# A mixture-of-experts product by two levels of Strassen-Winograd: VectorE's order by two clocks, weight sums made early

## The chip, the cores and the metric

The kernel runs on one core of a Trainium2 chip. Its metric is the time of one execution on the device in microseconds (us); less is better.

## The reference

Eight experts, 8192 tokens (16 x 512) of 512 features, 2048 outputs. Every token goes through every expert, and the outputs are added with softmax weights.

```python
probs = softmax(router_logits)                       # (16, 512, 8)
output = np.zeros((16, 512, 2048), np.float32)
for e in range(8):
    output += probs[:, :, e:e+1] * np.matmul(x, expert_weights[e])
```

The kernel reads this as one product: the left matrix has 8192 rows of 8 x 512 = 4096 columns (x times the probability of each expert), the right one stacks the experts, 4096 x 2048.

## The kernel before

**Two levels.** The product is split into halves in all three dimensions and done with seven products in place of eight (Winograd's form). The outer seven, P1 to P7, each have a right operand of 2048 x 1024 made from quarters of the weights: P1 takes the quarter 11, P2 21, P3 22, and P5, P6, P7, P4 take the outer sums t1, t2, t3, t4. The tokens make 16 instances: product(r, q) is outer product r of instance q. It is split again by seven (`STEPS` = 1, 5, 6, 2, 7, 3, 4). One *step* is one inner product: eight matmuls of 128 x 128 by 128 x 512 in f16, accumulated in one PSUM bank. So one outer product of an instance takes 7 steps, and needs seven right tiles of 1 MB in SBUF: three blocks of its operand as they are, and the inner sums 5, 6, 7 and 4 of its blocks (`inner_sums`, `sums_at`, one VectorE subtraction of 128 x 4096 each).

**Left operands.** VectorE makes each instance's left operands (`Left.make`): x transposed times a broadcast probability, a 128 x 2048 operation (tile `z`), for two halves; P6 subtracts P5's operand, P7 and P3 subtract two such products (`less`). `queue_s2` and `queue_i` add the inner left sums (tiles `d`, `z`).

**Evacuation.** After each step `post` moves a bank out: by ScalarE as a copy, by VectorE as an addition (`post_on_base`, 128 x 512, tile `h`). A base is an earlier partial result, held in `kept`, in the output in DRAM, or in SBUF, fetched by SyncE (`Base.fetch`). Results are stored by GpSimd's DMA queue; P4 and P3 add to the output by DMA.

**Stages.** `add` makes a stage of one or two products. `run` takes the steps of a pair in turn, so a pair has 14 slots and a single 7. Hooks put with `at(stage, slot, ...)` start loads and queue VectorE tasks. Before: three pairs of P1, eight of P2 with P1, four of P2, one of P5, a single P6, fourteen of P6 with P5, a single P6, a pair of P7, a single P4, fourteen of P4 with P7, a single P4, eight pairs of P3. The first two instances of P1 run ahead of the stages as plain products.

**The order.** Every engine runs its instructions in the order in which the Python code emits them. VectorE's tasks wait in `queue`. In each slot `slack` adds `SLOT` (1.73 us) to a credit and emits tasks while the credit is positive; a task's cost and an evacuation's 0.69 are taken off. If a step needs an operand that isn't made, `need` emits the queue up to it at once, and the credit goes below zero:

```python
def slack():
    credit[0] += SLOT
    while queue and credit[0] > 0:
        queue.popleft().run()
    credit[0] = min(credit[0], SLOT)
```

**Weights.** `cast_block` and `cast_w` load f32 weights as f16 on GpSimd's queue. `wedge` makes halves of t3, t1, t2 (and t4 of one block) from quarters 12 and 22 in the stages of P1 and P2 and stores them in DRAM (`kept_w`); their temporaries come from `zpool`. `retire` fetches the operand of P7, and of P3, in the last stages of the product before it and queues the four sums there; P4's sums are queued in P7's pair.

Of the kernel before, what the change touches and what calls it, by code (L numbers as in the profile page):

```python
# [31 lines left out]
def kernel(  # L32
# [8 lines left out]
    P = 128  # L41
# [22 lines left out]
    wpool = ctx.enter_context(tc.tile_pool(name="wpool", bufs=15))  # L64
    zpool = ctx.enter_context(tc.tile_pool(name="zpool", bufs=9))
    spool = ctx.enter_context(tc.tile_pool(name="spool", bufs=3))
# [64 lines left out]
    def new_w():  # L131
        return wpool.tile([P, K8, NB], f16, name="w", tag="w")

    def new_z():
        return zpool.tile([P, K8, HQ], f16, name="z", tag="z")
# [15 lines left out]
    def kept_w(what, kn):  # L151
        if (what, kn) not in stored:
            stored[what, kn] = dram.tile([P, K8, NB], f16, name=f"wd{what}_{kn[0]}{kn[1]}")
        return stored[what, kn]
# [178 lines left out]
    STEPS = (1, 5, 6, 2, 7, 3, 4)  # L333
    HP = HQ // 2
    queue = deque()
    credit = [0.0]

    class Task:
# [5 lines left out]
        def run(self):  # L344
            self.done = True
            credit[0] -= self.cost
            self.make()

    def need(task):
        while task is not None and not task.done:  # L350
            queue.popleft().run()

    def later(cost, make, first=False):
# [4 lines left out]
    def slack():  # L358
        credit[0] += SLOT
        while queue and credit[0] > 0:  # L360
            queue.popleft().run()
        credit[0] = min(credit[0], SLOT)

# [50 lines left out]
    class Left:  # L414
# [18 lines left out]
        def queue_make(self, k):  # L433
            cost = 1.22 + (2.33 if self.less is not None else 0) + (1.11 if self.of is not None else 0)
            self.task[k] = later(cost, lambda: self.make(k))

        def queue_s2(self):
            def make():
                self.s2 = spool.tile([P, K8, HP], f16, name="d", tag="d")
                tt(self.s2, self.t[0][:, :, ds(HP, HP)], self.t[0][:, :, ds(0, HP)], SUB)  # L440
            self.task["s2"] = later(0.58, make)

        def queue_i(self):
            def make():
                self.i = new_z()
                two = "p k (h t) -> p h k t"
                tt(self.i.rearrange(two, h=2), self.t[1].rearrange(two, h=2),
                   self.s2.unsqueeze(1).to_broadcast([P, 2, K8, HP]), SUB)
            self.task["i"] = later(1.15, make)

# [27 lines left out]
    class Product:  # L478
# [23 lines left out]
        def post_alone(self, p, x, q, b):  # L502
            o = self.o
            if p == 1:
                self.banks["b"] = bank()
                act(nc.scalar.copy(self.banks["b"], x))  # L506
            elif p in (5, 6):
                tn = (1, 1) if p == 5 else (0, 1)
                o[tn] = half()
                act(nc.scalar.copy(o[tn], q if p == 5 else x))  # L510
            elif p in (2, 4):
                o[TN[p]] = half()
                act(nc.scalar.copy(o[TN[p]], b if p == 2 else x))  # L513
            else:
                credit[0] -= 0.69
                tt(o[TN[p]], x if p == 7 else q, o[TN[p]], ADD)

        def post_on_base(self, p, x, q, b):
# [4 lines left out]
            if p == 2:  # L523
                act(nc.scalar.copy(o[tn], b))  # L524
                return
            credit[0] -= 0.69
            if p == 1:
# [71 lines left out]
    def product(r, q, **how):  # L599
# [7 lines left out]
        elif r == 2:  # L607
            if q >= 7:
# [86 lines left out]
    forget(*range(0, 14, 2))  # L695
    rest = [15, 0, 1, 2, 3, 4, 5, 6]
    for i in range(0, 8, 2):
        k = add(product(2, rest[i]), product(2, rest[i + 1]))
        for slot, tn in zip((8, 10, 12, 13), INNER):
            for q in rest[i:i + 2]:  # L700
                if q < 7:
                    fetch_at(k if tn == (1, 0) else k - 1, 3 if tn == (1, 0) else slot, bases[2, q], tn)
# [10 lines left out]
    for q in range(16):  # L713
# [7 lines left out]
    xs.clear()  # L721
    k7 = add(product(7, 0), product(7, 1))
    add(product(4, 0))
    for q in range(1, 15):
        add(product(4, q), product(7, q + 1))
    k4 = add(product(4, 15))
    for q in range(16):
        k = k7 if q < 2 else k7 + q
        for slot, tn in zip((7, 9, 11, 13) if len(stages[k - 1]) == 2 else (2, 3, 5, 6), INNER):
            fetch_at(k - 1, slot, bases[7, q], tn)  # L730
    xs.clear()
    for q in range(0, 16, 2):
        k3 = add(product(3, q), product(3, q + 1))


    def wedge(kn, e):
# [8 lines left out]

        def temp():
            return zpool.tile([P, C, NB], f16, name="z", tag="z")
# [13 lines left out]
        def t2():  # L761
            tt(b, b, a, ADD)
            send("t2", b)

        def t4():
            u = temp()
            tt(u, b21[kn][:, rows, :], b, SUB)
            send("t4", u)
        return casts, [t3, t1, t2] + ([t4] if kn == (0, 1) else [])

    def wedge_at(stage, slot, kn, e, then):
# [7 lines left out]
        def go_on():  # L779
            for make in made:  # L780
                later(1.11, make)
        at(stage, slot, begin)
        at(stage + then[0], then[1], go_on)

    b21 = {}
    made2 = {}

    def cast21(kn):
        b21[kn] = cast_block(21, kn)

    at(0, 0, lambda: cast21((0, 1)))
    wedge_at(0, 4, (0, 1), 0, (0, 13))
    at(0, 10, lambda: cast21((0, 0)))
    wedge_at(1, 2, (0, 1), 1, (1, 3))
    at(1, 6, lambda: cast21((1, 1)))
    at(1, 12, lambda: cast21((1, 0)))

    def sums_at(stage, slot, r, of, ps):
# [5 lines left out]
        at(stage, slot, go)  # L804
    sums_at(2, 5, 2, b21, (5, 6))
    sums_at(2, 10, 2, b21, (7, 4))
    for i, (kn, e) in enumerate((kn, e) for kn in ((0, 0), (1, 0), (1, 1)) for e in range(2)):
        wedge_at(3 + i, 2, kn, e, (0, 11))

    t1, t2, t3, t4, b22 = {}, {}, {}, {}, {}  # L810

    def fetch_at_w(stage, slot, of, what, kn):
        at(stage, slot, lambda: of.__setitem__(kn, fetch_w(what, kn)))
    for i, kn in enumerate(((0, 0), (0, 1), (1, 1), (1, 0))):
        fetch_at_w(11, 3 * i, t1, "t1", kn)
        fetch_at_w(12, 3 * i, t2, "t2", kn)
    last2 = k5 - 1
# [5 lines left out]

    def t4_at(stage, kn):
        def begin():
            t4[kn] = cast_block(21, kn)

        def go_on():
            def make():
                t = t4.pop(kn)  # L830
                tt(t, t, t2[kn], SUB)
                pool(kept_w("t4", kn), t)
            later(2.29, make)
        at(stage, 2, begin)
        at(stage + 1, 2, go_on)
    for i, kn in enumerate(((0, 0), (1, 0), (1, 1))):
        t4_at(k5 + 3 + 2 * i, kn)

    def retire(stage, r, of, fetch):

        order = ((0, 0), (0, 1), (1, 1), (1, 0))
        at(stage - 4, 2, lambda: fetch(order[0]))
        for slot, kn in zip((2, 4, 6), order[1:]):
            at(stage, slot, lambda kn=kn: fetch(kn))
        sums_at(stage, 13, r, of, (5, 6))
        sums_at(stage + 1, 2, r, of, (7, 4))
    retire(k7 - 2, 7, t3, lambda kn: t3.__setitem__(kn, fetch_w("t3", kn)))
    for i, kn in enumerate(((0, 0), (0, 1), (1, 1), (1, 0))):
        fetch_at_w(k7, 1 + i, t4, "t4", kn)
    sums_at(k7, 8, 4, t4, (5, 6))  # L850
    sums_at(k7, 11, 4, t4, (7, 4))
    retire(k4 - 1, 3, b22, lambda kn: b22.__setitem__(kn, cast_block(22, kn)))


    finish = products[3, 15]
    for q in (14, 15):
        p = products[3, q]
        p.base = bases[3, q] = Base(lambda tn, q=q: out_rows(q, 0, 1, tn))
        p.sink = lambda tn, o, q=q: sp(out_rows(q, 0, 1, tn), o)
        for slot, tn in zip((8, 10, 12, 13), INNER):  # L860
            fetch_at(k3 - 1, slot, p.base, tn)
    finish.steps = (1, 5, 6, 7, 3, 4, 2)
# [67 lines left out]
```

## Time and profile before

| | us |
|---|---|
| median of 3 runs | 1533.98 (1532.76 to 1534.71) |
| profiled execution | 1532.25 |
| its span, first to last instruction | 1530.4 |
| TensorE busy | 1406.5 (92%), 6390 matmuls |
| VectorE busy | 1109.0 (72%), 1252 instructions |
| ScalarE busy | 181.2 (12%) |
| GpSimd busy | 349.9 (23%) |

The DMA moved 303.91 MB, 199 GB/s on average. Busy times are shares of one execution, and matmuls overlap in the pipeline: their busy time says when TensorE had work, not how fast it went. In the page's slices each digit is a fortieth of the span, 38.3 us. PEclk is the clock that TensorE was granted. In lists of waits the columns are the sum in us, the number of waits and the longest; in a chain, the start, the length and what ran. L107 is the helper of every VectorE operation, L127 that of every matmul, L121 and L118 those of GpSimd's and SyncE's DMAs; so tiles tell more than lines.

### The profile page before, as it was taken

What the parts mean: (1) busy time and instruction counts of PE and PEld (TensorE: products, weight loads), DVE (VectorE), ACT (ScalarE), POOL (GpSimd) and SP (SyncE); (2) the same over time, 40 slices, a digit from 0 to 9 for tenths busy, and PEclk for the clock granted to TensorE, in tenths of its full rate; (3) what the DMA queues carried; (4) which work ended last, traced back from release to release, by engine and by line L of the source; (5) the groups of instructions that cost most, each with busy time, mean ns of one, the idle gap of its engine ahead of it and who ended that gap; (6) DMA issues with size and microseconds to landing.
All of it is one profiled execution on the core that took longest, in us unless ns stands there. A gap on an engine that the chain in (4) does not pass through costs nothing.

```text
span 1530.4 us, 17248 instructions
## 1 busy us (share of the span) xinstructions
PE 1406.5 (92%) x6390; PEld 627.5 (41%) x6390; DVE 1109.0 (72%) x1252; ACT 181.2 (12%) x314; POOL 349.9 (23%) x547
## 2 busy tenths in 40 slices
PE   9997999999999999999996667678999999789999
PEld 4443444444444444444442222223444444334444
DVE  5857776657788878787767454457998886779983
ACT  3211111100011111111110000000000000112220
POOL 3233332211212222212110101111212214122321
PEclk9998999999999999999998789899999999999999
DMA  9999989689668788766673334445878879678985
GB/s 198 226 296 251 244 265 221 207 304 318 218 191 243 226 240 224 245 212 202 204 262 127 135 83 103 117 117 138 204 203 193 219 186 190 130 126 183 200 171 124
DMA packets 180420, 303.91 MB, mean 199 GB/s; under 512 B 51056, under 2 KB 83056, under 8 KB 177904
## 3 DMA queue, kind: packets, MB, share of 16 engines
q0 software_dynamic: 79712, 163.09, 45.2%
q1 hardware_dynamic: 100624, 139.73, 30.4%
q8 instruction: 50, 0.82, 0.2%
q14 instruction: 34, 0.28, 0.1%
HBM read 185.11 MB, written 142.80 MB: 214 GB/s over the span
## 4 chain that ended last, share of the span: by engine, by line
PE 70%; issue 13%; DVE 10%; DMA 4%; POOL 3%; ACT 0%; POOLq 0%; DVEq 0%; ACTq 0%
PE ps L127 70%; DVE z L107 6%; POOL out_dram L121 2%; DMA w<-in_expert_weights_dram 2%; DVE h L107 2%; DVE w L107 1%; DMA kept<-h 1%; DMA wdt<-z 1%; DVE d L107 1%; POOL xs L121 0%; DMA h<-out_dram 0%; DMA out_dram<-h 0%; POOL w L121 0%; DMA h<-kept 0%; DVE ps L107 0%
## 5 line engine op out<-in xcount | busy, mean ns | idle before, releaser
L127 PE MATMUL ps<-w,z 128*128 128x512 f16 x5416 | 1212.5, 385 | 104.4 <-DVE z L107 82.4
L127 PEld LDWEIGHTS <-z 128*128 128x128 f16 x5416 | 534.7, 99 | 771.3 <-DVE z L107 96.5
L107 DVE TENSOR_TENSOR h<-ps,h 128x512 f32<-128x512 f32 x418 | 283.7, 688 | 328.1 <-PE ps L127 318.9
L121 POOL DMA_DIRECT2D out_dram<-h x376 | 243.8, 674 | 975.3 <-ACT h L524 478.3
L107 DVE TENSOR_TENSOR z<-xT,pT 128x2048 f16<-128x2048 f16 x284 | 339.3, 1218 | 10.1 <-DMA wdt<-z 6.2
L127 PE MATMUL ps<-w,d 128*128 128x512 f16 x880 | 201.8, 381 | 13.2 <-DVE d L107 6.9
L127 PEld LDWEIGHTS <-d 128*128 128x128 f16 x880 | 86.1, 98 | 120.1 <-DVE d L107 9.4
L107 DVE TENSOR_TENSOR z<-z,d 128x2048 f16<-128x2048 f16 x110 | 130.2, 1218 | 0.6 <-DMA wdt<-z 0.6
L107 DVE TENSOR_TENSOR z<-z 128x2048 f16<-128x2048 f16 x96 | 117.6, 1225 | 3.3
L524 ACT COPY h<-ps 128x512 f32<-128x512 f32 x65 | 38.1, 586 | 616.5 <-PE ps L127 615.3
L513 ACT COPY h<-ps 128x512 f32<-128x512 f32 x88 | 51.6, 587 | 382.8 <-PE ps L127 352.6
L107 DVE TENSOR_TENSOR w<-w 128x4096 f16<-128x4096 f16 (+1 forms) x47 | 90.0, 1925 | 0.7
L107 DVE TENSOR_TENSOR d<-z 128x1024 f16<-128x1024 f16 x110 | 75.6, 688 | 8.5 <-PE ps L127 6.3
L510 ACT COPY h<-ps 128x512 f32<-128x512 f32 x88 | 51.6, 586 | 175.1 <-PE ps L127 168.3
L107 DVE TENSOR_TENSOR ps<-ps,h 128x512 f32<-128x512 f32 (+1 forms) x67 | 45.8, 687 | 34.7 <-PE ps L127 32.9
L107 DVE TENSOR_TENSOR h<-h 128x512 f32<-128x512 f32 (+2 forms) x69 | 45.1, 675 | 0.1
L121 POOL DMA_DIRECT2D kept<-h x56 | 30.6, 547 | 50.9 <-DVE h L107 23.2
L121 POOL DMA_DIRECT2D w<-in_expert_weights_dram x47 | 35.5, 768 | 26.3 <-DMA w<-in_expert_weights_dram 11.7
L506 ACT COPY ps<-ps 128x512 f32<-128x512 f32 x44 | 25.1, 570 | 131.5 <-PE ps L127 131.1
L121 POOL DMA_DIRECT2D xs<-in_x_dram x30 | 21.5, 715 | 37.4 <-DMA x<-xT 25.6
L107 DVE TENSOR_TENSOR z<-w 128x2048 f16<-128x2048 f16 x10 | 12.2, 1219 | 13.2 <-DMA wdt<-z 10.1
L121 POOL DMA_DIRECT2D wdt<-w x19 | 10.2, 539 | 48.1 <-DVE w L107 48.1
(43 smaller groups left out, 60.9 us busy)
## 6 DMA issues: line engine op xcount, KB each, us to landing
out_dram<-h POOLq DMA_DIRECT2D x376, 256.0 KB, 4.7
pT<-p_dram SPq DMA_DIRECT2D x140, 256.0 KB, 5.2
h<-kept SPq DMA_DIRECT2D x92, 256.0 KB, 4.2
w<-in_expert_weights_dram POOLq DMA_DIRECT2D x45, 512.0 KB, 10.1
xT<-x SPq DMA_DIRECT2D x85, 256.0 KB, 4.9
h<-out_dram SPq DMA_DIRECT2D x72, 256.0 KB, 5.2
w<-wdt SPq DMA_DIRECT2D x16, 1024.0 KB, 10.0
kept<-h POOLq DMA_DIRECT2D x56, 256.0 KB, 4.7
```

The costliest lines, as they stand in the source:

```text
L107: dve(nc.vector.tensor_tensor(out=o, in0=a, in1=b, op=op))
L121: note(nc.gpsimd.dma_start(out=o, in_=i, **how))
L127: note(nc.tensor.matmul(ps, z, w, start=start, stop=stop, skip_group_check=True))
L506: act(nc.scalar.copy(self.banks["b"], x))
L510: act(nc.scalar.copy(o[tn], q if p == 5 else x))
L513: act(nc.scalar.copy(o[TN[p]], b if p == 2 else x))
L524: act(nc.scalar.copy(o[tn], b))
```

## The change

- The credit becomes two clocks, one for TensorE and one for VectorE. A slot moves TensorE's by 1.73; VectorE's tasks are emitted until its clock is within 0.3 (`LAG`) of TensorE's; neither clock falls behind the other's start, and a forced task moves TensorE's clock on.
- The inner sums of P7, P4 and P3 are made early and kept in DRAM: P7's whole (in a stage of P2), P4's and P3's in quarters (in stages of P6 with P5 and of P4 with P7). `turnover` then fetches seven tiles, one per pair of slots, each into the buffer of the product before whose step has just run.
- The stages: four pairs of P1, six of P2 with P1, five of P2, one of P5, a single P6, fourteen of P6 with P5, P6 with P7, fifteen of P4 with P7, P4 with P3, seven of P3, a single P3.
- Temporaries of the weights and of `less` have one buffer `u` of their own, and `zpool` 8 in place of 9. The block (0, 1) of t4 is made whole, from t2 kept in the buffer of quarter 11. The casts of quarter 21 and the wedges move to other slots.

```diff
-    zpool = ctx.enter_context(tc.tile_pool(name="zpool", bufs=9))
+    zpool = ctx.enter_context(tc.tile_pool(name="zpool", bufs=8))
...
+    def new_u():
+        return zpool.tile([P, K8, HQ], f16, name="u", tag="u", bufs=1)
...
+    LAG = 0.3
     queue = deque()
-    credit = [0.0]
+    clock = {"pe": 0.0, "dve": 0.0}
...
         def run(self):
             self.done = True
-            credit[0] -= self.cost
+            clock["dve"] += self.cost
             self.make()
 
     def need(task):
         while task is not None and not task.done:
             queue.popleft().run()
+            clock["pe"] = max(clock["pe"], clock["dve"])
...
     def slack():
-        credit[0] += SLOT
-        while queue and credit[0] > 0:
+        clock["dve"] = max(clock["dve"], clock["pe"])
+        clock["pe"] += SLOT
+        while queue and clock["dve"] < clock["pe"] - LAG:
             queue.popleft().run()
-        credit[0] = min(credit[0], SLOT)
+
+    def evacuated():
+        clock["dve"] = max(clock["dve"], clock["pe"]) + 0.69
...
             if self.less is not None:
-                u = new_z()
+                u = new_u()
...
-    for q in (2, 4, 6):
+    for q in (2, 4, 6, 8):
         add(product(1, q), product(1, q + 1))
-    for q in range(7, 15):
+    for q in range(9, 15):
         add(product(2, q), product(1, q + 1))
...
-    add(product(6, 15))
+    some = product(6, 15)
+    xs.clear()
+    k7 = add(some, product(7, 0))
+    for q in range(15):
+        add(product(4, q), product(7, q + 1))
+    some = product(4, 15)
+    xs.clear()
+    k3 = add(some, product(3, 0))
+    for q in range(1, 15, 2):
+        add(product(3, q), product(3, q + 1))
+    end = add(product(3, 15))
...
+        for slot, tn in zip((7, 9, 11, 17), INNER):
+            fetch_at(k7 + q - 1 + slot // 14, slot % 14, bases[7, q], tn)
...
         def t3():
-            u = temp()
+            u = new_u().rearrange("p (c two) t -> p c (two t)", two=2)
             tt(u, b, a, SUB)
             send("t3", u)
...
-    at(0, 0, lambda: cast21((0, 1)))
     wedge_at(0, 4, (0, 1), 0, (0, 13))
-    at(0, 10, lambda: cast21((0, 0)))
-    wedge_at(1, 2, (0, 1), 1, (1, 3))
-    at(1, 6, lambda: cast21((1, 1)))
-    at(1, 12, lambda: cast21((1, 0)))
+    at(0, 11, lambda: cast21((0, 1)))
+    wedge_at(1, 2, (0, 1), 1, (1, 11))
+    at(1, 8, lambda: cast21((0, 0)))
+    at(2, 2, early_t4)
+    at(2, 3, lambda: cast21((1, 1)))
+    at(2, 10, lambda: cast21((1, 0)))
...
-    sums_at(2, 5, 2, b21, (5, 6))
-    sums_at(2, 10, 2, b21, (7, 4))
+    sums_at(3, 1, 2, b21, (5,))
+    sums_at(3, 4, 2, b21, (6,))
+    sums_at(3, 7, 2, b21, (7,))
+    sums_at(3, 10, 2, b21, (4,))
...
+    def sums_in_place(part, b, r, cost):
+
+        def one(p, o, x, y):
+            def make():
+                tt(o, x, y, SUB)
+                part(p, o)
+            later(cost, make)
+        one(5, b[0, 0], b[0, 1], b[0, 0])
+        one(7, b[0, 1], b[1, 1], b[0, 1])
+        one(6, b[1, 1], b[1, 1], b[0, 0])
+        one(4, b[1, 0], b[1, 0], b[1, 1])
...
+    for i, kn in enumerate(ORDER):
+        fetch_at_w(10, 1 + 3 * i, t3, "t3", kn)
+        fetch_at_w(12, 1 + 3 * i, t1, "t1", kn)
+        fetch_at_w(13, 1 + 3 * i, t2, "t2", kn)
+    at(11, 2, lambda: whole_sums(7, t3))
...
+        t4_at(*slots_after(k5 + 2, 4, 20 * i), kn)
+    sums_by_parts(*slots_after(k5 + 2, 4, 62), 20, 4,
+                  lambda t, kn, j, chunks: sp(t, kept_w("t4", kn)[:, chunks, :]))
+    sums_by_parts(k7 + 4, 4, 36, 3, cast_part)
+
+
+    RAW = {1: (0, 0), 2: (1, 0), 3: (1, 1)}
+
+    def turnover(stage, place, r, raw):
+
+        right[r].w = {}
+
+        def fetch(p):
+            if p in RAW:
+                right[r].w[p] = raw(RAW[p])
+            else:
+                right[r].w[p] = new_w()
+                sp(right[r].w[p], kept_w((r, p), (0, 0)))
+        at(stage - 1, 9, lambda: fetch(1))
+        for i, p in enumerate(STEPS[1:]):
+            at(stage, place + 2 * i + 1, lambda p=p: fetch(p))
+    turnover(k7 - 1, 1, 7, lambda kn: fetch_w("t3", kn))
+    turnover(k7, 0, 4, lambda kn: fetch_w("t4", kn))
+    turnover(k3 - 1, 1, 3, lambda kn: cast_block(22, kn))
```

More of the change, by code (lines that the diff above doesn't have):

```diff
@@ L152, in kept_w @@
         if (what, kn) not in stored:
-            stored[what, kn] = dram.tile([P, K8, NB], f16, name=f"wd{what}_{kn[0]}{kn[1]}")
+            stored[what, kn] = dram.tile([P, K8, NB], f16, name="wd")
         return stored[what, kn]
@@ L433, in queue_make @@
         def queue_make(self, k):
-            cost = 1.22 + (2.33 if self.less is not None else 0) + (1.11 if self.of is not None else 0)
+            cost = 1.22 + (2.45 if self.less is not None else 0) + (1.23 if self.of is not None else 0)
             self.task[k] = later(cost, lambda: self.make(k))
@@ L440, in make @@
                 tt(self.s2, self.t[0][:, :, ds(HP, HP)], self.t[0][:, :, ds(0, HP)], SUB)
-            self.task["s2"] = later(0.58, make)
+            self.task["s2"] = later(0.69, make)
         def queue_i(self):
@@ L448, in make @@
                    self.s2.unsqueeze(1).to_broadcast([P, 2, K8, HP]), SUB)
-            self.task["i"] = later(1.15, make)
+            self.task["i"] = later(1.22, make)
         def op(self, p):
@@ L514, in post_alone @@
             else:
-                credit[0] -= 0.69
+                evacuated()
                 tt(o[TN[p]], x if p == 7 else q, o[TN[p]], ADD)
@@ L525, in post_on_base @@
                 return
-            credit[0] -= 0.69
+            evacuated()
             if p == 1:
@@ L607, in product @@
         elif r == 2:
-            if q >= 7:
+            if q >= 9:
                 base = products[1, q].o.__getitem__
@@ L688, in fetch_at @@
             at(stage, slot, lambda tn=tn: base.fetch(tn))
-    for q in (2, 4, 6):
+    for q in (2, 4, 6, 8):
         add(product(1, q), product(1, q + 1))
-    for q in range(7, 15):
+    for q in range(9, 15):
         add(product(2, q), product(1, q + 1))
-    forget(*range(0, 14, 2))
-    rest = [15, 0, 1, 2, 3, 4, 5, 6]
-    for i in range(0, 8, 2):
+    forget(*range(0, 18, 2))
+    rest = [15] + list(range(9))
+    for i in range(0, 10, 2):
         k = add(product(2, rest[i]), product(2, rest[i + 1]))
@@ L700 @@
             for q in rest[i:i + 2]:
-                if q < 7:
+                if q < 9:
                     fetch_at(k if tn == (1, 0) else k - 1, 3 if tn == (1, 0) else slot, bases[2, q], tn)
@@ L720 @@
             at(*where, lambda q=q, tn=tn: joined(q, tn))
[L721 to L733, printed above, removed]
+        for slot, tn in zip((7, 9, 11, 17), INNER):
+            fetch_at(k7 + q - 1 + slot // 14, slot % 14, bases[7, q], tn)
     def wedge(kn, e):
@@ L744, in casts @@
             cast_w(22, kn, e, b)
-        def temp():
-            return zpool.tile([P, C, NB], f16, name="z", tag="z")
         def send(what, u):
@@ L761, in t2 @@
         def t2():
[L762 to L769, printed above, removed]
+            if kn == (0, 1):
+                tt(b11[kn][:, rows, :], b, a, ADD)
+                send("t2", b11[kn][:, rows, :])
+            else:
+                tt(b, b, a, ADD)
+                send("t2", b)
+        return casts, [t3, t1, t2]
     def wedge_at(stage, slot, kn, e, then):
@@ L780, in go_on, with early_t4 @@
             for make in made:
-                later(1.11, make)
+                later(1.22, make)
         at(stage, slot, begin)
-        at(stage + then[0], then[1], go_on)
-    b21 = {}
-    made2 = {}
+        at(*then, go_on)
+    b21, t1, t2, t3 = {}, {}, {}, {}
     def cast21(kn):
         b21[kn] = cast_block(21, kn)
-    at(0, 0, lambda: cast21((0, 1)))
-    wedge_at(0, 4, (0, 1), 0, (0, 13))
-    at(0, 10, lambda: cast21((0, 0)))
-    wedge_at(1, 2, (0, 1), 1, (1, 3))
-    at(1, 6, lambda: cast21((1, 1)))
-    at(1, 12, lambda: cast21((1, 0)))
+    def early_t4():
+        kn = 0, 1
+        def make():
+            t = new_w()
+            tt(t, b21[kn], b11[kn], SUB)
+            pool(kept_w("t4", kn), t)
+        later(2.29, make)
+    wedge_at(0, 4, (0, 1), 0, (0, 13))
+    at(0, 11, lambda: cast21((0, 1)))
[4 more added lines that the diff above has]
+    at(2, 10, lambda: cast21((1, 0)))
     def sums_at(stage, slot, r, of, ps):
@@ L804, in sums_at, with make, whole_sums @@
         at(stage, slot, go)
-    sums_at(2, 5, 2, b21, (5, 6))
-    sums_at(2, 10, 2, b21, (7, 4))
+    sums_at(3, 1, 2, b21, (5,))
+    sums_at(3, 4, 2, b21, (6,))
+    sums_at(3, 7, 2, b21, (7,))
+    sums_at(3, 10, 2, b21, (4,))
     for i, (kn, e) in enumerate((kn, e) for kn in ((0, 0), (1, 0), (1, 1)) for e in range(2)):
-        wedge_at(3 + i, 2, kn, e, (0, 11))
-    t1, t2, t3, t4, b22 = {}, {}, {}, {}, {}
+        wedge_at(4 + i, 2, kn, e, (4 + i, 11))
     def fetch_at_w(stage, slot, of, what, kn):
         at(stage, slot, lambda: of.__setitem__(kn, fetch_w(what, kn)))
-    for i, kn in enumerate(((0, 0), (0, 1), (1, 1), (1, 0))):
-        fetch_at_w(11, 3 * i, t1, "t1", kn)
-        fetch_at_w(12, 3 * i, t2, "t2", kn)
+    ORDER = ((0, 0), (0, 1), (1, 1), (1, 0))
+    def sums_in_place(part, b, r, cost):
+        def one(p, o, x, y):
+            def make():
+                tt(o, x, y, SUB)
[5 more added lines that the diff above has]
+        one(4, b[1, 0], b[1, 0], b[1, 1])
+    def whole_sums(r, b):
+        sums_in_place(lambda p, o: pool(kept_w((r, p), (0, 0)), o), b, r, 2.29)
+    for i, kn in enumerate(ORDER):
[3 more added lines that the diff above has]
+    at(11, 2, lambda: whole_sums(7, t3))
     last2 = k5 - 1
@@ L822 @@
     sums_at(k5, 8, 6, t2, (7, 4))
[L824 to L835, printed above, removed]
-    for i, kn in enumerate(((0, 0), (1, 0), (1, 1))):
[L837 to L852, printed above, removed]
-    finish = products[3, 15]
[L856 to L861, printed above, removed]
+    def slots_after(stage, slot, n):
+        slot += n
+        while slot >= 7 * len(stages[stage]):
+            slot -= 7 * len(stages[stage])
+            stage += 1
+        return stage, slot
@@ new lines, in t4_at, with make, sums_by_parts, begin @@
+    def t4_at(stage, slot, kn):
+        t = []
+        def make():
+            tt(t[0], t[0], t2[kn], SUB)
+            pool(kept_w("t4", kn), t.pop())
+        at(stage, slot, lambda: t.append(cast_block(21, kn)))
+        at(*slots_after(stage, slot, 11), lambda: later(2.29, make))
+    def sums_by_parts(stage, slot, every, r, load):
+        for j in range(4):
+            b, chunks = {}, ds(2 * j, 2)
+            def begin(b=b, j=j, chunks=chunks):
+                t = new_w()
+                for i, kn in enumerate(ORDER):
+                    b[kn] = t[:, ds(2 * i, 2), :]
+                    load(b[kn], kn, j, chunks)
+            def go_on(b=b, chunks=chunks):
+                sums_in_place(lambda p, o: pool(kept_w((r, p), (0, 0))[:, chunks, :], o), b, r, 0.69)
+            at(*slots_after(stage, slot, j * every), begin)
+            at(*slots_after(stage, slot, j * every + 8), go_on)
@@ new lines, in cast_part @@
+    def cast_part(t, kn, j, chunks):
+        k, n = kn
+        pool(t, expert_weights[HE + 2 * k + j // 2, ds(j % 2 * 2 * P, 2 * P),
+                               ds(NH + n * NB, NB)].rearrange("(c p) n -> p c n", p=P))
+    for i, kn in enumerate(((0, 0), (1, 0), (1, 1))):
+        t4_at(*slots_after(k5 + 2, 4, 20 * i), kn)
+    sums_by_parts(*slots_after(k5 + 2, 4, 62), 20, 4,
+                  lambda t, kn, j, chunks: sp(t, kept_w("t4", kn)[:, chunks, :]))
+    sums_by_parts(k7 + 4, 4, 36, 3, cast_part)
@@ new lines @@
+    RAW = {1: (0, 0), 2: (1, 0), 3: (1, 1)}
[4 more added lines that the diff above has]
+                right[r].w[p] = raw(RAW[p])
+            else:
+                right[r].w[p] = new_w()
[4 more added lines that the diff above has]
+    turnover(k7 - 1, 1, 7, lambda kn: fetch_w("t3", kn))
@@ L862 @@
+    turnover(k7, 0, 4, lambda kn: fetch_w("t4", kn))
+    turnover(k3 - 1, 1, 3, lambda kn: cast_block(22, kn))
+    finish = products[3, 15]
+    finish.base = Base(lambda tn: out_rows(15, 0, 1, tn))
+    finish.sink = lambda tn, o: sp(out_rows(15, 0, 1, tn), o)
+    for slot, tn in zip((6, 8, 10, 12), INNER):
+        fetch_at(end - 1, slot, finish.base, tn)
     finish.steps = (1, 5, 6, 7, 3, 4, 2)
```

## The prediction

> **What bounds the kernel now.** I read the page's slices first: TensorE, VectorE, the granted clock.
>
> ```profile
> PE   9997999999999999999996667678999999789999
> DVE  5857776657788878787767454457998886779983
> PEclk9998999999999999999998789899999999999999
> ```
>
> Both engines sag together in slices 22 to 28, so neither is the bound there. Then the table of busy time by stretch (length; busy time and count of TensorE, its weight loads, VectorE, ScalarE, GpSimd; granted clock; DMA share; GB/s):
>
> ```profile
> 65.80:91.70 25.90, 24.27 (x113) 10.91 (x112) 16.61 (x17) 5.83 (x10) 9.68 (x16) 1.00 1.14 297
> 91.70:128.30 36.60, 25.99 (x114) 11.38 (x113) 22.36 (x19) 5.83 (x10) 9.29 (x17) 0.86 1.09 282
> 128.30:442.50 314.20, 314.20 (x1457) 142.41 (x1456) 222.72 (x251) 38.52 (x66) 84.29 (x147) 1.00 0.86 247
> 783.40:810.20 26.80, 24.53 (x114) 10.98 (x113) 18.67 (x21) 2.35 (x4) 5.95 (x11) 1.00 0.74 259
> 810.20:1069.00 258.80, 176.58 (x674) 69.79 (x673) 141.66 (x154) 6.45 (x11) 31.08 (x45) 0.85 0.43 117
> 1069.00:1286.50 217.50, 217.50 (x1009) 98.60 (x1008) 188.18 (x221) 10.55 (x18) 57.08 (x80) 1.00 0.80 196
> 1286.50:1406.00 119.50, 101.03 (x450) 44.43 (x449) 89.80 (x88) 18.66 (x32) 27.65 (x34) 0.96 0.75 151
> ```
>
> Call eight matmuls of one inner product a step. Thirteen pairs of 14 steps took 314.2 us with TensorE always busy: 24.17 us a pair, 1.726 a step, no loss. All 770 steps are 55 pairs. So each stretch has a loss: 41.6 to 128.3 us holds three pairs, 86.7 - 72.5 = 14.2; 442.5 to 469.2 one, 2.5; 783.4 to 810.2 one, 2.6; 810.2 to 1069 six, 258.8 - 145.0 = 113.8; 1286.5 to 1406 four, 22.8. Together 155.9 of the span's 1530.4; with none, 1374.5. Of the 113.8, idling is 82.2 (258.8 - 176.6); the other 31.6 is matmuls at a low clock (176.6 - 145.0).
>
> Now the waits in 810.2 to 1069, and a piece of the chain there:
>
> ```profile
> DVE h L107 <- PE ps L127: 89.2, 52, 4.3
> PE ps L127 <- DVE z L107: 67.5, 23, 6.7
> ```
>
> ```profile
> 857.07 0.69 DVE h L107
> 857.76 1.14 DVE z L107
> 858.91 0.04 issue
> 858.95 1.92 PE ps L127 x8
> ```
>
> VectorE waits for TensorE to evacuate a bank, makes the next operand only behind that, and TensorE waits for it: two engines in turn. The cause is the order in which the program puts VectorE's instructions. Its credit goes negative when operands are forced, and until it is repaid nothing is made ahead.
>
> **The change, part by part.** *VectorE's order.* I walked the compiled order of both kernels. For each step I took the VectorE instruction that makes its operand or frees its bank, and the evacuations ahead of it. Work from an evacuation to the operand was priced by the trace's spacing when VectorE is not waiting (0.60 us an evacuation or half operand, 1.14 a 2048-wide one, 2.20 a whole weight sum; above, 857.76 to 858.91 is one 1.14) and set against 1.726 us for each step TensorE has in between. Before, 59 steps come out late: 44 in the 810-to-1069 stretch, 9 in 1286-to-1406, 4 at 783-to-810, 2 at 442-to-469, where the waits are; none elsewhere. One late pair there (from 959 us) has seven late steps of 2.4, 1.8, 1.8, 1.8, 5.9, 2.4 and 2.0, 18.1 in all; it took 43.10 against 24.17, 18.9. So the count prices well. In the changed order two steps are late: 1.9 us soon after the single of P6 (3.7 of work against 1.73), and 0.7 in the last product. Of the 141.7 us in those four stretches (2.5 + 2.6 + 113.8 + 22.8), 2.6 stays.
>
> *Weight sums.* Twelve whole sums (12 x 2.20 = 26.4 us) at the turnovers become 4 whole and 32 quarter sums (8.8 + 32 x 0.60 = 28.0) in stages with room. What hides them: a pair of P4 and P7 has 19.9 us of VectorE work by these spacings, 22.3 with four quarter sums; a pair of P2 15.3, 24.1 with P7's four. Both stay under 24.17 (one group of 14 steps reaches 24.4, beside one of 17.7); an excess that lasts would be lost pair by pair. Taken: 0.
>
> *Their DMA.* Each of P7, P4 and P3 gets about 11 MB more (stores, loads of sums, and a second read of sources), 33 on 304. The dense spot is P7's turnover: the stage before its pair with P6 issues 7 loads of 1024 KB, 8 stores, 7 base loads and 6 operand loads of 256 KB, 12.25 MB; the next stage 6 loads and 18 transfers, 10.5. That is 23.9 million bytes in 48.3 us. Two stretches show what the DMA can carry, and the page the latencies:
>
> ```profile
> 345.80:370.00 24.20, 24.20 (x114) 10.95 (x113) 15.84 (x20) 1.17 (x2) 4.40 (x9) 1.00 0.99 370
> 325.00:330.00 5.00, 5.00 (x25) 2.25 (x23) 4.62 (x6) 0.00 (x0) 0.00 (x0) 1.00 1.03 419
> ```
>
> ```profile
> h<-out_dram SPq DMA_DIRECT2D x72, 256.0 KB, 5.2
> w<-wdt SPq DMA_DIRECT2D x16, 1024.0 KB, 10.0
> ```
>
> At 419 GB/s the two stages take 57.0 us, 8.7 too long; at 370, 64.6 and 16.3. A weight is fetched 15 steps (25.9 us) ahead and lands in 10.0 or so: 15.9 to spare, enough. The base loads of P7 stand in the same SyncE queue only 8 steps (13.8 us) ahead: 8.6 to spare, so at 370 GB/s they come up to 7.7 late. VectorE's evacuation, and every operand behind it in its order, would wait; TensorE feels it after about three steps (5.2 us). Ends: 0 (8.7 just fits) and 16.3 (the whole backlog); I take 4, nearer to the row of 419, since the fetches are large.
>
> Here a rule speaks against the change. The Trainium skill, "DMA: Bandwidth & Descriptors", Specifications, gives some 358 GB/s as the HBM limit of a core; by it the two stages would take 66.8 us and the estimate for this term would be 18.5. The stretch of 345.8 to 370 ran at 370 without any loss, and 419 was seen, so the trace speaks for less.
>
> Four stages of P2 now carry 9.0 to 9.5 MB each (P7's sums, then t1 and t2): 38.3 million bytes in 96.7 us, 396 GB/s. At 419 nothing is lost, at 370 6.8; I take 1.5, as a light stage (3.5 MB) follows. P3's turnover: as many bytes as before (8.75 MB against 7.75 a stage), where the walk explains all the loss; 1, ends 0 and 5.
>
> *The start.* Waits in 91.7 to 128.3:
>
> ```profile
> DVE z L107 <- DMA wdt<-z: 10.8, 2, 10.1
> PE ps L127 <- DVE h L107: 10.6, 1, 10.6
> ```
>
> An operand's buffer was still being stored as a weight temporary, VectorE stood 10.1 us, and TensorE 10.6 behind it. The change gives the temporary a buffer of its own, so this wait goes. It also spreads the casts (four per stage, not six in one) and starts P2 a stage later. What is late next: the DMA stays full (share 1.14 and 1.09), and the second wedge's casts have 9 steps, 15.5 us, to land, against a median of 13.0 between 40 and 135 us in this trace. If they are late, VectorE stands at t3 with evacuations behind it. Ends: 0 and 14.2 (as before); I take 3. Two casts leave the prologue; TensorE was busy 38.7 of its 41.6 us, so at most 1 us is gained: 0 taken, 1 kept for the low end. The pool of operands shrinks from 9 to 8, but the temporaries that shared it left: 0.
>
> *Clock.* The slow stretch ran at 0.85 with idle gaps up to 6.7 us; at 448 us a gap of 2.3 left it at 1.00 (442.5 to 469.2 lost no more than that). Single gaps of 1.9 and 0.7 therefore cost only themselves. The skill's "TensorE: Matmul & The Clock Gate", Part 1, has half rate after an idle window of about 3.4 us; by it too these two would cost nothing more, while a DMA wait of 5 us would bring, as an estimate, 1.7 us on top.
>
> **Sum.** 1374.5 + 2.6 + 4 + 1.5 + 1 + 3 = 1386.6 us of span. The profiled execution took 1532.25 for a span of 1530.4, 1.85 around it; the median, 1533.98, is 1.73 above it. So 1386.6 + 3.6 = 1390.2.
>
> **Rivals.** *DMA pays it back at P7's turnover:* base loads late by the whole 16.3 instead of 4: 1402. For it: 12.25 MB in one stage was never tried. Against: 419 GB/s. *The start stays as it was* (14.2 in place of 3): 1401. For it: share 1.14 there. Against: the wait named is on a buffer that goes. *The order does not hold:* the clocks count no DMA wait, so one late load sets VectorE behind its evacuations again; six pairs at 18.1 are 109 more: 1499. Against: the new clocks forgive debt, so the next pair starts even. *Slower than before:* the same alternation, but lasting in the 29 pairs of P4, P7 and P3, where VectorE is fullest (19.6 to 24.4 of 24.17) and has least room to catch up; 18.1 a pair, so from nine pairs on the gain is gone; at twelve, 1390 + 217 = 1607. Against: 1069 to 1286, with the same 20 us of work a pair, lost nothing once it was even.
>
> **Chances.** Forecast 0.63 (1379 to 1396), turnover 0.15, start 0.12, order not held 0.07, slower 0.03. The range: low, all DMA terms at 0 and 1 gained at the prologue, 1374.5 + 2.6 - 1 + 3.6 = 1379.7; high, all at their upper ends, 1374.5 + 2.6 + 16.3 + 6.8 + 5 + 14.2 + 3.6 = 1423. That leaves out 0.10. A difference under 0.2%, 3 us, can't be told from none: faster 0.96, same 0.01, slower 0.03.
>
> **What would show it.** Right: the stretch from 800 us on at 24.17 a pair, clock 1.00, and hardly any wait of TensorE for z. Wrong: waits for z in P4 and P7 pairs (order), waits of VectorE for h from out_dram at P7's turnover (DMA), or of TensorE before 130 us (start). A time over 1425 would mean that the walk missed a wait.

## The result, and the profile after

The changed kernel took 1418.01 us (median of four runs, 1416.24 to 1419.3) against 1533.74: a ratio of 0.9245, interval 0.9229 to 0.9261. The forecast was 1390, range 1379 to 1423. The profiled execution took 1416.24 for a span of 1414.4.

The slices of TensorE, VectorE and the granted clock no longer sag in the middle:

```profile
PE   8998999999989999999999899999999999899998
DVE  4956767669679888887877688888888986798882
PEclk9999999999999999999999999999999999999999
```

The table by stretch, cut where steps were lost (columns as before):

```profile
91.20:123.60 32.40, 26.09 (x114) 11.36 (x113) 20.24 (x20) 5.84 (x10) 10.24 (x17) 0.95 1.16 279
389.50:419.90 30.40, 26.03 (x113) 11.39 (x112) 21.49 (x23) 1.17 (x2) 3.30 (x7) 0.94 0.89 301
444.00:470.70 26.70, 24.51 (x114) 10.84 (x112) 25.32 (x31) 2.92 (x5) 5.74 (x10) 1.00 1.01 239
784.90:817.30 32.40, 26.69 (x114) 11.48 (x112) 20.94 (x27) 1.76 (x3) 4.34 (x8) 0.89 0.98 380
817.30:1180.70 363.40, 362.77 (x1682) 164.35 (x1680) 316.07 (x377) 17.62 (x30) 107.66 (x156) 1.00 0.86 228
1180.70:1240.60 59.90, 51.31 (x226) 22.47 (x224) 44.47 (x48) 8.17 (x14) 14.67 (x19) 0.94 1.00 249
1240.60:1409.90 169.30, 168.52 (x786) 76.63 (x784) 129.45 (x132) 37.40 (x64) 48.26 (x56) 1.00 0.79 159
```

The fifth row is what the change did: fifteen pairs of P6, P4 and P7 in 363.40 us, 24.23 a pair, where six took 258.8 before. The other rows are what stayed. The first four hold one pair of 24.17 each and the sixth two, so they lost 8.2, 6.2, 2.5, 8.2 and 11.6 us. With 0.8 each at 66 to 91 and 841 to 866, and 0.9 in the last product (in the last row, where TensorE idles for 0.8), that is 39.2 of the span, against 155.9 before.

VectorE's waits for a DMA tell what most of them are (sum in us, number, longest):

```profile
DVE h L107 <- DMA out_dram<-h: 15.8, 7, 7.6
DVE z L107 <- DMA xT<-xs: 14.8, 3, 6.3
DVE h L107 <- DMA h<-kept: 9.9, 1, 9.9
DVE ps L107 <- DMA h<-kept: 9.9, 2, 8.7
DVE h L107 <- DMA h<-out_dram: 8.9, 2, 6.9
```

Beside these it waits 217 times for a bank from TensorE (199.7 us, which cost nothing while TensorE is busy), 10.9 us for ScalarE before the stages begin, and twice near 100 us, which the profile puts down to issue (7.6) and to TensorE (6.6); both are taken up below, under the start. TensorE's wait for z, 67.5 us before in the slow stretch alone, is down to one of 2.2, at P6's single.

### The profile page after: what moved, and what is told of

Same layout as the page of the kernel before. It is cut to its first block, busy times and chain, and to the rows that moved or that the text cites. A ratio compares the mean times of both kernels' runs of the same rounds, so it can differ in the third digit from the quotient of the medians.

```text
span 1414.4 us, 17403 instructions
## 1 busy us (share of the span) xinstructions
PE 1377.9 (97%) x6390; PEld 624.0 (44%) x6390; DVE 1105.4 (78%) x1271; ACT 183.8 (13%) x318; POOL 383.8 (27%) x600
## 4 chain that ended last, share of the span: by engine, by line
PE 81%; DMA 11%; DVE 3%; issue 2%; SPq 1%; POOL 1%; ACT 0%; DVEq 0%; POOLq 0%; ACTq 0%
PE ps L127 81%; DMA h<-kept 3%; DMA w<-in_expert_weights_dram 2%; DMA xT<-xs 2%; DMA out_dram<-h 2%; DMA h<-out_dram 1%; SPq L393 1%; DVE h L107 1%; DVE z L107 1%; DMA xs<-in_x_dram 1%; DMA xT<-x 1%; DMA w<-wd 1%; POOL w L121 0%; DVE w L107 0%; POOL out_dram L121 0%
## 5 line engine op out<-in xcount | busy, mean ns | idle before, releaser
L127 PE MATMUL ps<-w,z 128*128 128x512 f16 x5416 | 1182.6, 380 | 17.8 <-DVE h L107 15.4
L121 POOL DMA_DIRECT2D out_dram<-h x380 | 248.6, 679 | 838.0 <-ACT h L532 433.6
L107 DVE TENSOR_TENSOR z<-xT,pT 128x2048 f16<-128x2048 f16 x220 | 267.1, 1218 | 21.3 <-DMA xT<-xs 14.8
L127 PE MATMUL ps<-w,d 128*128 128x512 f16 x880 | 203.1, 384 | 11.6 <-DVE ps L107 11.6
L107 DVE TENSOR_TENSOR w<-w 128x1024 f16<-128x1024 f16 (+2 forms) x72 | 96.0, 1336 | 0.5
L107 DVE TENSOR_TENSOR z<-z,u 128x2048 f16<-128x2048 f16 x64 | 78.4, 1225 | 2.2
L107 DVE TENSOR_TENSOR u<-xT,pT 128x2048 f16<-128x2048 f16 x64 | 78.0, 1219 | 0.0
L121 POOL DMA_DIRECT2D w<-in_expert_weights_dram x61 | 46.1, 775 | 31.3 <-PE ps L127 11.6
L107 DVE TENSOR_TENSOR h<-h 128x512 f32<-128x512 f32 (+2 forms) x69 | 45.0, 675 | 11.7 <-DMA h<-kept 9.9
L121 POOL DMA_DIRECT2D wd<-w x56 | 31.3, 559 | 39.3 <-DVE w L107 32.2
L107 DVE TENSOR_TENSOR z<-z 128x2048 f16<-128x2048 f16 x32 | 39.2, 1225 | 1.1
```

The lines of the kernel that those rows point to most:

```text
L107: dve(nc.vector.tensor_tensor(out=o, in0=a, in1=b, op=op))
L121: note(nc.gpsimd.dma_start(out=o, in_=i, **how))
L127: note(nc.tensor.matmul(ps, z, w, start=start, stop=stop, skip_group_check=True))
```

## The experiments

In the table, the us lost to the 24.17 cadence at each place, from each kernel's one profiled execution, and the median of its runs. The column of P2 counts all from 300 to 420 us; the 0.9 of the last product is left out.

| kernel | start | P2, 300-420 | P6 single | to P7 and P4 | to P3 | median |
|---|---|---|---|---|---|---|
| before | 14.1 | 0 | 2.5 | 116.4 | 22.7 | 1533.7 |
| changed | 9.0 | 6.2 | 2.5 | 9.0 | 11.6 | 1418.0 |
| clocks only | 11.7 | 0 | 2.5 | 17.4 | 12.2 | 1421.9 |
| old credit | 9.8 | 7.4 | 2.5 | 8.7 | 12.8 | 1420.6 |
| singles | 7.9 | 6.9 | 2.5 | 9.0 | 15.6 | 1421.6 |
| singles, old credit | 9.4 | 8.0 | 2.5 | 9.5 | 11.7 | 1419.7 |
| bases first | 8.6 | 1.5 | 5.0 | 8.8 | 12.3 | 1414.4 |
| raw f16 | 7.4 | 6.6 | 2.5 | 9.1 | 0 | 1403.9 |
| ScalarE's queue | 8.9 | 6.7 | 2.5 | 5.1 | 8.8 | 1407.5 |
| start | 11.6 | 6.9 | 2.5 | 9.0 | 11.8 | 1418.7 |
| three together | 6.5 | 7.6 | 2.5 | 5.4 | 5.6 | 1405.4 |
| three and start | 12.8 | 4.2 | 2.5 | 4.8 | 5.2 | 1409.5 |
| three and P7's bases | 7.4 | 5.5 | 4.1 | 8.1 | 5.6 | 1408.2 |
| bases first, raw f16 | 8.6 | 2.1 | 3.3 | 8.8 | 0 | 1401.0 |

**Which part brought it.** Four kernels undo or do single parts. The clocks, with the task costs of after (0.07 to 0.12 us higher each), in the kernel before; from the edit:

```diff
...
     def slack():
-        credit[0] += SLOT
-        while queue and credit[0] > 0:
+        clock["dve"] = max(clock["dve"], clock["pe"])
+        clock["pe"] += SLOT
+        while queue and clock["dve"] < clock["pe"] - LAG:
             queue.popleft().run()
-        credit[0] = min(credit[0], SLOT)
...
```

> The kernel before with the two clocks (and the changed task costs) alone; singles, late weight sums and the start stay as they were. Theory A, the one on record: the credit's debt is the cause, so the two clocks bring most of the gain. The walk over this kernel's order still leaves 25 late steps with 47.9 us, at the turnovers to P7 and P4 (17.3 and 12.6) and to P3 (11.6), where 171 us were late before. So 1534 - 141.7 + 48 = 1440 us, somewhat more where gaps over 3 us bring the half clock, say 1440 to 1460. Theory B, the sums at the turnovers are the cause whatever the order: little gained, over 1490.

Measured 1421.91, ratio to before 0.9272 (0.9253 to 0.9291). The clocks bring nearly all of the gain, more than theory A's 1440 to 1460 gave them. The stretch in which before lost 116 us, and TensorE's wait for z from 800 to 1250 us:

```profile
808.80:871.80 63.00, 50.85 (x226) 21.94 (x224) 57.68 (x59) 1.76 (x3) 8.34 (x13) 0.95 0.62 198
871.80:1186.10 314.30, 314.30 (x1458) 142.47 (x1456) 270.37 (x318) 15.25 (x26) 79.86 (x112) 1.00 0.76 192
```

```profile
PE ps L127 <- DVE z L107: 23.1, 8, 7.3
```

At the turnover VectorE is busy 57.7 of 63.0 us: the sums fill it, TensorE waits for z, and then it is over. Before, the alternation went on for four more pairs. The Python code of before gives the course of its credit: it falls to -12.5 us, stays below zero from P6's last single to the sixth pair of P4 with P7, and tasks are forced in each stage from P7's pair to the fourth of these pairs. With the higher task costs and the old credit it would fall to -13.8 and stay below zero for longer, so the costs aren't what helped.

The reverse, the changed kernel with the old credit (the same edit turned around, with the task costs of before):

> The changed kernel with the credit and the task costs of before in place of the two clocks; early sums, pairs and the start as changed. Theory A (the credit's debt is the cause): the alternation comes back, 1480 us or more. Theory B (the sums at the turnovers are what makes the debt, and without them either order does): the walk finds 3 late steps with 3.4 us against 2 with 2.6, so within 5 us of 1418.

Measured 1420.61, ratio to before 0.9264 (0.9245 to 0.9284). Theory A falls in the form that went on record: with the sums out of the turnovers the credit, by the code, never falls below -3.4 us, is back at its upper bound of 1.73 within every pair from P6 with P7 on, and forces no task there. TensorE waits for VectorE nowhere between 820 and 1182 us:

```profile
819.70:1182.60 362.90, 362.79 (x1682) 164.37 (x1680) 316.29 (x379) 17.58 (x30) 107.73 (x156) 1.00 0.88 228
```

Then the pairs. The stages of before from P6 on, first with the clocks, then with the credit too:

```diff
-    some = product(6, 15)
+    add(product(6, 15))
     xs.clear()
-    k7 = add(some, product(7, 0))
-    for q in range(15):
+    k7 = add(product(7, 0), product(7, 1))
+    add(product(4, 0))
+    for q in range(1, 15):
         add(product(4, q), product(7, q + 1))
...
```

> The changed kernel with the stages of before from P6 on (single P6, a pair of P7, single P4 at both ends, eight pairs of P3); clocks, early sums and the start as changed. If the pairs in the middle matter by VectorE's order: the walk finds 9 late steps with 13.5 us against 2.6, so 1418 + 11 = 1429. If what matters there is the DMA at the turnovers, it goes the other way: with a whole stage more between fetch and use the stalls of 8 us at P7's and 11 us at P3's turnover shrink, and the sum stays near 1418 or falls below.

> The singles of before and the credit of before, with the early weight sums (and the start) of the change: what the early sums do without the other two. Walk: 10 late steps with 12.2 us. Theory B (early sums alone are the gain): 1418 to 1432. Theory A: 1480 us or more.

Measured 1421.61 and 1419.70 (ratios 0.9265 and 0.9254, intervals 0.9248 to 0.9283 and 0.9233 to 0.9275). So the singles cost nothing that can be told; the stalls at the turnovers didn't shrink either (9.0 and 15.6 us, for 9.0 and 11.6 in the changed kernel). And the early sums (with the changed start), with credit and singles, bring the gain as well. Clocks and early sums are two remedies for one loss: either takes the alternation away, and the second finds little left. In exchange, the early sums bring DMA: the clocks-only kernel loses nothing at 390 to 420 us.

**What the changed kernel still loses.** Four kernels change one thing each. Base loads of one stage ahead of the transposes:

```diff
-        for slot, tn in zip((8, 10, 12, 13), INNER):
+        for slot, tn in zip((2, 4, 5, 6) if i == 8 else (8, 10, 12, 13), INNER):
```

> The changed kernel; in the last stage but one before P5's pair (the stage of P2's instances 5 and 6) the eight base loads are put at slots 2, 4, 5, 6 in place of 8, 10, 12, 13, ahead of the transposes of P5's x in SyncE's queue. Theory: the 6.2 us lost at 390 to 420 us come from base loads that stood behind transposes, which stood 20.4 us for x to land. Then that loss goes, and 1418 becomes 1412. Rival: the DMA engines are full there (9 to 9.5 MB a stage) and any order in the queue loses the same: 1418, the loss at another step.

Measured 1414.35, and 1.5 us lost there in place of 6.2: the order in SyncE's queue was the cause. The seven kernels of the table with the early sums and without this edit lost 6.2 to 8.0 there; of the whole times the intervals just overlap (0.9203 to 0.923, and 0.9229 to 0.9261). Some of it came back at P6's single (5.0 for 2.5). The reason named was not quite right. SyncE's issues in the changed kernel, and VectorE's wait there:

```profile
376.70 12.27 SPq L393 DMA_TRANSPOSE xT<-xs  x4
...
389.72 2.25 SPq L118 DMA_DIRECT2D h<-kept  x4
```

```profile
DVE ps L107 <- DMA h<-kept: 8.7, 1, 8.7
```

SyncE was busy for 12.3 us with issuing four transposes whose x had landed, and the base loads behind them came late, 10.4 us after issue. The wait of 20.4 us for x is another: it began at 407.8 us, when the loss was over.

P3's raw blocks as f16 from DRAM:

```diff
+    def copy_raw(stage, kn, e):
+        at(stage, 8, lambda: cast_w(22, kn, e, kept_w("raw", kn)[:, ds(e * C, C), :]))
+    for stage, (kn, e) in zip((1, 2, 3, 5, 8, 10), ((kn, e) for kn in RAW.values() for e in range(2))):
+        copy_raw(k7 + stage, kn, e)
...
-    turnover(k3 - 1, 1, 3, lambda kn: cast_block(22, kn))
+    turnover(k3 - 1, 1, 3, lambda kn: fetch_w("raw", kn))
```

> The changed kernel; the three blocks of quarter 22 that P3 takes as they are, are cast from DRAM to DRAM in six earlier stages of P4 with P7, and fetched at the turnover as f16 on SyncE's queue, in place of casts on GpSimd's. Theory: at P3's turnover VectorE stands 7.6 us for stores of P7's results that land 21 us late behind the casts in GpSimd's queue, and TensorE loses 11.6 us from there on. Without casts there, that loss falls to 0 to 4 us: 1407 to 1411. Rival: the turnover loses by its bytes, seven loads in a stage, as P7's does (8.2 us on SyncE's queue): 1414 or more.

Measured 1403.89. The chain of the changed kernel at that place (start, length, what):

```profile
1191.37 0.47 POOL w L121
...
1192.87 0.07 POOL out_dram L121
...
1193.44 21.48 DMA out_dram<-h
...
1215.02 0.70 DVE h L107
```

A store of a P7 result (256 KB, median 6.2 us in this kernel) is issued behind casts of 512 KB and lands after 21.5 us; VectorE can't add P4's part into that tile before. A wait of 6.9 us for a base load on SyncE's queue went before it and cost 1.7 of the 11.6. Without the casts, two and a half pairs from there on (1179 to 1239) run without a gap; the first row is the first two of them:

```profile
1179.00:1227.35 48.35, 48.35 (x225) 21.91 (x224) 41.96 (x46) 8.16 (x14) 12.66 (x16) 1.00 0.98 292
1179.00:1239.00 60.00, 60.00 (x279) 27.20 (x278) 53.44 (x59) 9.92 (x17) 17.26 (x22) 1.00 0.98 278
```

The share of the DMA is as high as in the changed kernel (0.98, 1.00), and more is moved in a microsecond (278 GB/s, 249), so the bytes alone were not the limit. But two things changed. The stores no longer stand behind casts (they land after 16.4 us at most), and the engines have less to do: two pairs took them 47.4 us of time (0.98 of 48.35), for 59.9 with the casts (1.00 of 59.90), at nearly the same bytes (14.1 and 14.9 MB). Whether the order of the queue or the time of the casts counted for more isn't shown.

The 1 MB loads on a queue of their own:

```diff
+    def aq(o, i):
+        act(nc.scalar.dma_start(out=o, in_=i))
...
-        sp(t, stored[what, kn])
+        aq(t, stored[what, kn])
...
-                sp(right[r].w[p], kept_w((r, p), (0, 0)))
+                aq(right[r].w[p], kept_w((r, p), (0, 0)))
```

> The changed kernel with every load of a 1 MB weight tile from DRAM issued by ScalarE in place of SyncE. Theory: at P7's turnover the base loads of P6 landed 16 us after issue because they stood behind 1 MB loads in one queue; in a queue of their own they land in 6 to 8 us, and the 8.2 us at 785 to 817 (and perhaps the 6.2 at 390 to 420) go: 1404 to 1410. Rival: the DMA engines are full (12.25 MB in a stage), the queues share them, and the loss stays: 1415 to 1420; or ScalarE waits for buffers in order and its copies come late: slower than 1418.

Measured 1407.45: 5.1 lost at P7's turnover for 9.0, 8.8 at P3's for 11.6, no change at 390 to 420. At P7's, P6's base load still comes late: VectorE stands 7.5 us for it, not 9.9. In the changed kernel the chain there was:

```profile
789.96 16.08 DMA h<-kept
```

On a queue without 1 MB loads, the load that VectorE waits for was issued at 785.4 us, 4.6 earlier, and landed after 18.4: not sooner after its issue, but later. So the time fits the theory and the landing fits the rival, the engines that the queues share; what the second queue gave here is the earlier issue.

The start:

```diff
-    wedge_at(1, 2, (0, 1), 1, (1, 11))
+    wedge_at(1, 2, (0, 1), 1, (2, 2))
...
-    at(2, 10, lambda: cast21((1, 0)))
+    at(3, 2, lambda: cast21((1, 0)))
...
```

> The changed kernel; the last cast of quarter 21 is moved from stage 2 to stage 3, P2's sums behind it, and the sums of the second half of the wedge start at stage 2 slot 2 in place of stage 1 slot 11 (the early block of t4 four slots later). Theory: the 9 us lost before 125 us are casts and x landing late in a full GpSimd queue, VectorE standing in order behind them. With 2 casts fewer before 115 us and the wedge given 5 slots more, 3 to 6 of the 9 us go: 1412 to 1415. Rival: what is late is x alone (transposes), and the same is lost: 1418.

Measured 1418.66: the rival. TensorE lost 11.6 us before 126 us, and VectorE's wait there is x alone:

```profile
DVE z L107 <- DMA xT<-xs: 22.4, 3, 10.8
```

**Put together.** The first three in one kernel, and that with one more edit each:

> The changed kernel with the base loads ahead of the transposes, quarter 22 cast from DRAM to DRAM early, and the 1 MB loads on ScalarE's queue. If the three losses are separate (they lie in different stages), the gains add: 3.7 + 14.1 + 10.6 less what the second and third share at P3's turnover (2 to 4 us): 1392 to 1396. If a freed place only moves the DMA's backlog to the next: 1400 or more.

> As the one with three, and at the start the first half of the wedge's casts goes to stage 1 slot 8, the second to stage 3, P2's casts to stages 0 and 2: two casts fewer before the end of stage 2, none between x's load of stage 1 and its transposes. Theory: what TensorE loses there (8 us, at step 11 of the third group) is x for stage 3, late in a full DMA; with room there 4 to 8 us go. Rival: the transposes themselves are slow (13 us for four) whatever else runs: same as the one with three.

The edit of the second at the start:

```diff
-    wedge_at(0, 4, (0, 1), 0, (0, 13))
-    at(0, 11, lambda: cast21((0, 1)))
-    wedge_at(1, 2, (0, 1), 1, (1, 11))
-    at(1, 8, lambda: cast21((0, 0)))
-    at(2, 2, early_t4)
+    at(0, 4, lambda: cast21((0, 1)))
+    at(0, 11, lambda: cast21((0, 0)))
+    wedge_at(1, 8, (0, 1), 0, (2, 3))
     at(2, 3, lambda: cast21((1, 1)))
     at(2, 10, lambda: cast21((1, 0)))
+    wedge_at(3, 2, (0, 1), 1, (3, 11))
+    at(3, 13, early_t4)
...
```

and of the third at P7's turnover:

```diff
-        for slot, tn in zip((7, 9, 11, 17), INNER):
+        for slot, tn in zip((12, 13, 14, 17) if q == 0 else (7, 9, 11, 17), INNER):
```

> As the one with three, and in P7's turnover the base loads of P7's first instance stand behind those of P6's last (slots 12, 13, 14, 17 in place of 7, 9, 11, 17). Theory: with weights in a queue of their own, P6's base loads are still late (5 us lost) because P7's take the buffers and the place before them: that 5 us goes, 3 to 5 us less than the one with three. Rival: the bytes of that stage are the limit: the same.

Measured 1405.37, 1409.51 and 1408.17: the gains don't add. With three, 7.2 us are lost at 390 to 420 again (VectorE stands 3.5 us for a base and 5.4 for an operand), and 5.6 at P3's turnover, where f16 blocks on SyncE's queue left none (9.2 for a base). With the start changed, 5.1 are lost at the old place, but 7.8 at 144 to 176, where P2 begins. With P7's bases later, the loss leaves 784 to 813 and comes back at 809 to 865 (8.1), after waits of 2.2 and 3.1 us for P7's bases and one of 7.7 for a store. In the last two a wait only changed its place.

So the queue was put back and the other two kept:

> The changed kernel with the base loads ahead of the transposes and quarter 22 cast early, and the 1 MB loads on SyncE's queue as in the changed kernel. With the loads on ScalarE's queue the first of these lost its effect (7.2 us at 388 to 419 again, where 1.5 was left without). If that was the queue's doing, both gains add here: 1418.0 - 3.7 - 14.1 = 1400.2, the fastest of all. If gains at one place of the DMA are given back at another: 1403 to 1406.

Measured 1400.98 in five runs, ratio to before 0.9136 (0.9123 to 0.9148), the fastest: 17 us below the changed kernel. By place both gains add on SyncE's queue (2.1 us at P2, none at P3); by the time, the interval just overlaps that of the f16 blocks alone (0.9139 to 0.9171). On ScalarE's queue the first was lost and the second halved, and why its loads disturb these stages was not followed further.

## Why the prediction was right or wrong

The time fell into the range, but the forecast of 1379 to 1396, held the likeliest, was missed by 22 us.

- **No loss, 1374.5.** Right: 1414.4 less the 39.2 is 1375.2.
- **VectorE's order, 2.6 left.** Right in size and place: 2.5 after P6's single and 0.9 in the last product, where the walk had 1.9 and 0.7, and none else. The reason given was half of it. The credit's debt does carry the alternation on, but it is made where sums and operands crowd at the turnovers, and the kernels with the old credit show that moving the sums is enough. The prediction priced clocks and sums as one step and did not ask what each does alone.
- **The walk's price.** It counts late steps well (waits stand where it has them); their sum held at P3's turnover in the clocks-only kernel (11.6, measured 12.2), but not at those to P7 and P4 (29.9, measured 17.4). Perhaps a delay once paid also moves the next step; that wasn't followed.
- **Start, 3 (0 to 14.2).** Too low: 9.0. The buffer wait did go (no wait of z for a weight store is left). What came next was the wedge's cast, as priced (VectorE stood 7.6 us for it in the changed kernel, 2.0 of them paid by TensorE), and a second wait of 6.6 us, which the profile puts down to TensorE. It was x: the last transpose of that x, issued at 95.2 us, landed after 17.2, at 112.5, and VectorE went on at 112.7. The transposes of that window landed after 15.0 us (median), 8.5 in the same window before, and the start kernel names x at this place. Both edits of the start only moved the loss, so what would remove it stays open.
- **P2's four stages, 1.5 (0 to 6.8).** Too low: 6.2. The loss came not from the rate but from a queue: SyncE took 12.3 us to issue four transposes, with the next base loads behind.
- **P7's turnover, 4 (0 to 16.3).** Too low: 9.0 with what followed. The mechanism was nearly as told: base loads came late among the 1 MB loads, landing after 16.1 us. They were P6's last ones, not P7's, and VectorE came to the late one 6.2 us after its issue (16.1 less the wait of 9.9), not the 13.8 that were priced for P7's. From 785 to 834 us the DMA carried 374 GB/s, but 407 from 790 to 812, while that load was under way: the step that was mis-sized is the time to spare, not the rate. By the 358 GB/s of the Trainium skill ("DMA: Bandwidth & Descriptors", Specifications) the term was estimated at 18.5, twice what was lost; the 407 show that this figure wasn't the limit here.
- **P3's turnover, 1 (0 to 5).** Wrong, outside its ends: 11.6. The step that failed was to judge it by bytes, and to take the loss before as all the walk's. P7's stores stand behind casts in GpSimd's queue, and P4 adds into the tiles being stored: one landed after 21.5 us and VectorE stood 7.6 for it. Without casts there, nothing was lost.
- **The clock.** Right for the short gap: a wait of 2.2 us at P6's single left it at 1.00. After waits of 5.7 and 7.0 us the next two steps cost 1.6 and 0.7 to 0.9 more, 2.4 and 2.5 on top. The estimate drawn from the Trainium skill's "TensorE: Matmul & The Clock Gate", Part 1, was 1.7.
- **Rivals.** None came alone; the likeliest forecast was missed because four DMA terms, each taken near its low end, were all high: 36 together, not 9.5. All four lie where the DMA was near full (shares of 0.89 to 1.16), so they were hardly independent; that this is their one cause isn't shown, as two of them went with edits to the order in a queue or the casts alone. P3's term went beyond its own end, and that the time still fell into the range is owed to the width of the other three: so far it was luck.

## What to carry to other kernels

When a stall shows two engines in turn, ask what filled the queue and what kept it full: removing either may do, and undoing one part at a time tells whether the rest is worth its cost. When traffic is added to a nearly full DMA, follow each in-order queue: what stands behind the large transfer, and which engine waits for that; lead time in steps says little once a landing takes three times its median. Where several terms hang on one nearly full DMA, don't take each near its low end: here all four came out high.

## What the runs showed of the hardware that was not expected

A 256 KB store behind two 512 KB casts on GpSimd's queue landed after 21.5 us (median of such stores 6.2 in that kernel, 4.7 before); without the casts, at more bytes per second, such stores landed after 16.4 at most there. A 256 KB load on a queue without 1 MB loads still landed after 18.4 us while 1 MB loads ran on another. DMA transposes landed after 15.0 us (median) between 66 and 125 us of the changed kernel, against 5.6 over the whole of it. Single waits of TensorE of 5.7 and 7.0 us were followed by 2.4 and 2.5 us more at a low clock, one of 4.5 by 1.5, one of 2.2 by none.
